# Eight adaLN tiles taken from the first layer's down projection and given to the second layer's gates and attention projection

## The chip, the core and the metric

The kernel runs on one core of a Trainium2 chip. The metric is device microseconds from the start to the end of one execution, the median of several runs. The profile is of one further execution of the same program.

## What is computed

Two layers of a decoder trunk on one sequence of 256 tokens with 1024 channels. Cut to what matters here:

```python
c_act = jax.nn.silu(c)                                   # (1, 1024)
for l in range(2):
    mod = c_act @ w_ada[l] + b_ada[l]                    # 6144 numbers out of a 1024 x 6144 matrix
    sh1, sc1, gt1, sh2, sc2, gt2 = split(mod, 6)
    h = rms_norm(x, norm_mix[l]) * (1 + sc1) + sh1
    proj = h @ w_in[l]
    # proj's columns: gated-DeltaNet q, k, v, z, a, b; attention q, k, v; gate_a; gate_b
    y_a = delta_net(...) @ w_dn_out[l]
    y_b = sliding_window_attention(...) @ w_swa_out[l]
    merged = sigmoid(gate_a) * y_a + sigmoid(gate_b) * y_b
    x = x + gt1 * (merged @ w_o[l])
    h = rms_norm(x, norm_ffn[l]) * (1 + sc2) + sh2
    up_act, up_lin = split(h @ w_up[l], 2)
    up_act = causal_dwconv(up_act, ffn_conv[l]) + ffn_conv_b[l]
    x = x + gt2 * ((silu(up_act) * up_lin) @ w_down[l])
```

All of it is float32. The line `mod = c_act @ w_ada[l] + b_ada[l]` is the adaLN modulation: six groups of 1024 numbers in each layer, which depend on `c` alone and so may be computed at any time before they are used. Groups 0 to 5 are `sh1, sc1, gt1, sh2, sc2, gt2`.

## The kernel before

**Weights.** Channels lie on the 128 partitions, tokens in the free dimension. All weights are streamed once from HBM in chunks of 128 x 1024 float32 (512 KB; 432 KB for the attention's own columns; an output tile's weights of the down projection come as three chunks, of 1024, 1024 and 768 columns). A float32 product is made of three TensorE matmuls in `float32r` (`mm3`, L262 to L265): high part times high part, high times low, low times high. So each chunk is first split: it lands in a buffer `raw`, ScalarE copies it to the high part `wH` (L192), VectorE subtracts to make the low part `wL` (L193). `emit_chunk` (L182) does this, and `weights` (L198) keeps it three chunks ahead of the chunk that TensorE multiplies (`LOOK = 3`). There are six `raw` buffers (L111), four `wH`, four `wL`.

**adaLN tiles.** `w_ada` of a layer is cut into 48 tiles of 128 x 1024 (512 KB each), eight to a group. A tile is not multiplied on TensorE: `ada_fetch` (L304) loads it into a buffer `raw` of the same six that the weights use, and `ada_dot` (L301) is one VectorE instruction (L302), which multiplies it by `silu(c)` and sums each row into one column of `modp`. After each fourth tile `ada_cols` (L319) adds the bias and makes the factors that are used later (L322 to L328). `ada_step(n)` (L337) does `n` such tiles: it issues the next loads from the list `adaq` until two are in flight, and emits the oldest one's dot product.

**When the tiles are done.** A table of numbers sets how many tiles go beside which piece of the main work. Layer 0's first 16 tiles are done at the start (`ada_first`), the other 32 in its mixer. Layer 1's 48 are done in this order: 16 in layer 0's channel sub-layer, one beside each of the hidden tiles 4 to 19 (`FST`, `FSN`, L1161); then `WDN[f]` of them beside output tile `f` of layer 0's down projection (L1176); then `ADC[1]`, nine in all, beside layer 1's convolved heads (L1060); then `GST[1]` beside each of its gate tiles (L1067); and one beside each of its attention-projection tiles (L1086), as long as the list has any:

```python
        def gate(q, f):
            ...
            ada_step(GST[l])
...
            if l + 1 < NL:
                ada_step(WDN[f])
```

Layer 1 has 12 gate tiles beside its mixer (four of `gate_a`, eight of `gate_b`; the first four of `gate_a` are done before). Groups 2 to 4 must be complete before layer 1's output projection (L1100), group 5 before its down projection (L1162).

**Order.** Each engine runs its instructions in one fixed order. It is set when the program is built: a scheduler takes instructions by priority (`tc.high_priority(offset=...)`, higher first) and by its own estimate of when each could start. The weights' splits stand above the dot products. All loads of weights and adaLN tiles are issued by SyncE's one queue, in order, and each waits there until its buffer `raw` is free, which is when the VectorE instruction that reads the buffer's last contents has run.

**The stages around the change.** Layer 0's down projection (L1165 to L1181): for each of eight output tiles, 22 blocks of the hidden vector (`g_a`, `g_b`) times three matmuls, from three chunks; then VectorE updates `x` (L1174), adds to the sum of squares (L391), and splits the next layer's input (L405). Layer 1's mixer from its gates on (L1071 to L1086): the delta rule of the second four heads (`chain_b`: a triangular inverse in steps `ps_y`, `ps_z`, then `ps_S`, `ps_KS`), and four attention units (`ps_cur`, `ps_prv`: scores; `s`, `mx`, `es`, `sme`: softmax; `ps_pT`, `pc`: transposed weights; `ps_o`: output), all woven between the matmuls of the 12 gate tiles. The attention projection (`sH`, `sL`; L1081 to L1086) can do only its first four blocks before the last attention unit is done.

Of the kernel before, what the change touches and what calls it, by code (L numbers as in the profile page):

```python
# [37 lines left out]
AHEAD = 1000  # L38
HPC = (4000, 4000)
ADC = ((2, 3, 2, 2), (3, 1, 3, 2))  # L40
GST = (1, 2)
FST = (4, 4)
FSN = ((1, 1), (1, 1))
WDN = (0, 3, 3, 3, 3, 3, 1, 0)
HPN = 20000
HPE = (500, 2000)
LAST = 2
# [52 lines left out]
def trunk(tc, xT, cvec, pos, wada, wsa, wbig, wdn, par, cst, out):  # L100
# [236 lines left out]
    def ada_step(n=1):  # L337

        for _ in range(n):
            while adaq and len(adaf) < 2:  # L340
                l, g, f = adaq.pop(0)
                adaf.append((l, g, f, ada_fetch(l, g * 8 + f)))
            if adaf:
                l, g, f, raw = adaf.pop(0)
                dot = ada_dot(l, g * 8 + f, raw)
                if behind:
                    after(dot, behind["op"])
                if f % 4 == 3:
                    ada_cols(l, g, f - 3, f + 1)
# [142 lines left out]
    for l in range(NL):  # L492
# [568 lines left out]
        def gate(q, f):  # L1061
# [3 lines left out]
            with tc.high_priority(offset=HPN):  # L1065
                A.activation(q[f // 4][:, f % 4], p_, AF.Tanh, scale=0.5)
            ada_step(GST[l])  # L1067

# [96 lines left out]
        for f in range(8):  # L1165
# [9 lines left out]
            if l + 1 < NL:  # L1175
                ada_step(WDN[f])  # L1176
                with tc.high_priority(offset=HPN):
# [92 lines left out]
```

## Time and profile before

| | us |
|---|---|
| median of 3 runs (lowest, highest) | 1035.65 (1034.38, 1040.53) |
| the profiled execution's own time | 1033.2 |
| its span (first to last instruction) | 1031.4 |
| TensorE busy | 992.9 |
| VectorE busy | 851.2 |
| ScalarE busy | 629.4 |
| adaLN dot products from `raw`, 80 of them, on VectorE | 96.9 |

Times in the trace are counted from the span's start. A row of a group says how many instructions it holds, how long the engine was busy with them, the mean of one in ns, how long the engine had stood idle just before them, and what ended the idle time. PE is TensorE, DVE VectorE, ACT ScalarE, SP SyncE, SPq its queue of DMA issues. Matmuls overlap: each takes 276 ns or so, but one starts about every 114 ns.

### The profile page before, as it was taken

How to read it: one execution, taken by the hardware profiler on the slowest of the kernel's cores; microseconds unless marked ns; L12 is line 12 of the kernel's file. 1: busy time of each engine (PE TensorE's matmuls, PEld its weight loads, DVE VectorE, ACT ScalarE, POOL GpSimd, SP SyncE). 2: the span in 40 equal slices, each digit the busy share in tenths (PEclk: the TensorE clock that was granted, in tenths of full speed). 3: DMA queues.
4: the chain of work that ended last, by engine and by line, in shares of the span. 5: the costliest groups of instructions: out<-in, count | busy, mean ns of one | idle time of the engine just before them, and what ended most of it. 6: DMA issues, size and time to landing. Idle time of an engine off the chain costs nothing.

```text
span 1031.4 us, 23285 instructions
## 1 busy us (share of the span) xinstructions
PE 992.9 (96%) x9248; PEld 950.7 (92%) x9248; DVE 851.2 (83%) x1907; ACT 629.4 (61%) x1261; POOL 4.0 (0%) x8
## 2 busy tenths in 40 slices
PE   3899999999999999999999999999999999999998
PEld 1799998997999999998999999989878999999998
DVE  6999998799788899897996999986957889777653
ACT  5389766756545675564465897667564558555532
POOL 0000000000000000000000000000000000000000
PEclk9999999999999999999999999999999999999999
DMA  9864676547566578888976547772323665666661
GB/s 358 344 225 132 228 266 223 184 136 233 161 200 186 160 230 284 272 288 260 338 286 207 169 145 224 239 252 83 97 70 103 193 195 169 198 189 196 181 211 44
DMA packets 60013, 210.48 MB, mean 204 GB/s; under 512 B 6784, under 2 KB 7808, under 8 KB 59904
## 3 DMA queue, kind: packets, MB, share of 16 engines
q1 hardware_dynamic: 59616, 208.72, 61.2%
q8 instruction: 72, 1.18, 0.5%
q14 instruction: 37, 0.30, 0.1%
q10 hardware_dynamic: 288, 0.28, 0.1%
HBM read 207.92 MB, written 1.05 MB: 203 GB/s over the span
## 4 chain that ended last, share of the span: by engine, by line
PE 66%; DVE 19%; DMA 5%; ACT 5%; issue 4%; SPq 0%; ACTq 0%; DVEq 0%
PE acc L263 18%; PE acc L264 17%; PE acc L265 17%; DVE wL L193 6%; DMA raw<-wada 4%; DVE raw L302 2%; ACT wH L192 2%; DVE kq L627 2%; DVE early L302 2%; PE pa L540 1%; PE pa L541 1%; PE ps_o L986 1%; PE ps_kk L683 1%; PE pa L539 1%; DVE vv L627 1%
## 5 line engine op out<-in xcount | busy, mean ns | idle before, releaser
L192 ACT CAST wH<-raw 128x1024 fp32r<-128x1024 f32 (+2 forms) x302 | 308.9, 1029 | 220.3 <-PE acc L264 129.8
L193 DVE TENSOR_TENSOR wL<-raw,wH 128x1024 fp32r<-128x1024 f32 (+2 forms) x302 | 359.3, 1195 | 78.0 <-ACT wH L192 75.3
L263 PE MATMUL acc<-hH,wH 128*128 128x256 f32 x1376 | 393.4, 286 | 0.0
L264 PE MATMUL acc<-hL,wH 128*128 128x256 f32 x1376 | 384.4, 279 | 0.0
L265 PE MATMUL acc<-hH,wL 128*128 128x256 f32 x1376 | 383.3, 279 | 0.0
L263 PEld LDWEIGHTS acc<-hH,wH 128*128 128x128 f32 x1376 | 258.6, 188 | 7.5 <-issue 4.1
L264 PEld LDWEIGHTS acc<-hL,wH 128*128 128x128 f32 x1376 | 258.7, 188 | 0.5
L265 PEld LDWEIGHTS acc<-hH,wL 128*128 128x128 f32 x1376 | 258.8, 188 | 0.2
L302 DVE SCALAR_TENSOR_TENSOR raw<-raw,cact 128x1024 f32<-128x1024 f32 x80 | 96.9, 1217 | 15.7 <-DMA raw<-wada 15.7
L265 PE MATMUL acc<-g_b,wL 128*128 128x256 f32 x224 | 62.3, 278 | 0.9 <-DVE wL L193 0.9
L263 PE MATMUL acc<-g_b,wH 128*128 128x256 f32 x224 | 62.0, 277 | 0.0
L264 PE MATMUL acc<-g_b,wH 128*128 128x256 f32 x224 | 62.0, 277 | 0.0
L627 DVE SCALAR_TENSOR_TENSOR kq<-cr,pt,kq 128x255 f32<-128x255 f32 (+2 forms) x96 | 45.5, 475 | 0.5 <-ACT kq L625 0.4
L265 PEld LDWEIGHTS acc<-g_b,wL 128*128 128x128 f32 x224 | 42.1, 188 | 1.3 <-DVE wL L193 1.3
L263 PEld LDWEIGHTS acc<-g_b,wH 128*128 128x128 f32 x224 | 42.0, 188 | 0.0
L264 PEld LDWEIGHTS acc<-g_b,wH 128*128 128x128 f32 x224 | 42.0, 188 | 0.0
L1147 DVE SCALAR_TENSOR_TENSOR g<-acc,pt,g 128x255 f32<-128x255 f32 x80 | 38.2, 477 | 0.6
L265 PE MATMUL acc<-g_a,wL 128*128 128x256 f32 x128 | 35.7, 279 | 2.8 <-DVE wL L193 2.8
L263 PE MATMUL acc<-sH,wH 128*128 128x256 f32 x128 | 36.6, 289 | 0.0
L265 PE MATMUL acc<-sH,wL 128*128 128x256 f32 x128 | 36.5, 287 | 0.0
L264 PE MATMUL acc<-sL,wH 128*128 128x256 f32 x128 | 36.3, 285 | 0.0
L540 PE MATMUL pa<-wL,hH 128*128 128x432 f32 x88 | 32.3, 369 | 3.7 <-DVE wL L193 3.7
(327 smaller groups left out, 1961.7 us busy)
## 6 DMA issues: line engine op xcount, KB each, us to landing
raw<-wbig SPq DMA_DIRECT2D x232, 512.0 KB, 4.1
raw<-wada SPq DMA_DIRECT2D x80, 512.0 KB, 4.5
raw<-wdn SPq DMA_DIRECT2D x32, 512.0 KB, 4.3
raw<-wsa SPq DMA_DIRECT2D x24, 432.0 KB, 6.9
early<-wada SPq DMA_DIRECT2D x16, 512.0 KB, 9.3
raw<-wdn SPq DMA_DIRECT2D x16, 384.0 KB, 4.0
x<-xT SPq DMA_DIRECT2D x4, 256.0 KB, 4.9
out<-x SPq DMA_DIRECT2D x8, 128.0 KB, 2.9
```

What stands on the lines that cost most here:

```text
L192: A.copy(h, raw)
L193: V.tensor_tensor(lo, raw, h.bitcast(F32), ALU.subtract)
L263: PE.matmul(o, wh, ah, start=first, stop=False)
L264: PE.matmul(o, wh, al, start=False, stop=False)
L265: PE.matmul(o, wl, ah, start=False, stop=last)
L302: return V.scalar_tensor_tensor(raw, raw, 1.0, cact, op0=ALU.mult, op1=ALU.mult, accum_out=modp[l][:, f:f + 1])
L539: PE.matmul(o, hh[:, kt, sl], wh[:, k4], start=kt == 0, stop=False)
L540: PE.matmul(o, hh[:, kt, sl], wl[:, k4], start=False, stop=False)
L541: PE.matmul(o, hl[:, kt, sl], wh[:, k4], start=False, stop=kt == KT - 1)
L627: V.scalar_tensor_tensor(dst[:, sft:], cr[:, :T - sft], w_[:, 3 - sft:4 - sft], dst[:, sft:], op0=ALU.mult, op1=ALU.add)
L683: PE.matmul(pk_[:, ch], t[:, 0, cs_], t[:, :, cs_], start=True, stop=True)
L1147: V.scalar_tensor_tensor(g[:, sft:], pa_[:, :T - sft], fw[:, i, 2 - sft:3 - sft], g[:, sft:], op0=ALU.mult, op1=ALU.add)
```

## The change

Two entries of the table change. Nothing else in the program's text does.

```diff
-GST = (1, 2)
+GST = (1, 1)
 FST = (4, 4)
 FSN = ((1, 1), (1, 1))
-WDN = (0, 3, 3, 3, 3, 3, 1, 0)
+WDN = (0, 1, 2, 1, 2, 1, 1, 0)
```

`WDN` now sums to 8 instead of 16, so that 24 of layer 1's tiles instead of 16 are left for its mixer. Nine of them still go beside the convolved heads. Of the others there were 7, two beside each of the first gate tiles; now there are 15, one beside each of the 12 gate tiles and one beside each of the first three tiles of the attention projection. The same 48 tiles are loaded and summed, with the same instructions.

The order in which the built program holds its instructions moves at three places. First VectorE in layer 0's down projection, at its second and third output tile (`modp_105` is layer 1's, L302 a dot product, L1174 the end of an output tile). Before:

```order
L302 SCALAR_TENSOR_TENSOR raw,modp_105<-raw,cact 128x1024 x2
L193 TENSOR_TENSOR wL<-raw,wH 128x1024
L322 TENSOR_TENSOR mod_103<-modp_105,pt 128x4
L328 TENSOR_SCALAR gt1h_112<-mod_103 128x4
L193 TENSOR_TENSOR wL<-raw,wH 128x768
L1174 SCALAR_TENSOR_TENSOR x<-acc_6461,mod_102,x 128x256
L302 SCALAR_TENSOR_TENSOR raw,modp_105<-raw,cact 128x1024
L391 TENSOR_TENSOR ssq<-ssq,sqx 128x256
L405 SCALAR_TENSOR_TENSOR xL<-x,a_1_108,xH 128x256
L193 TENSOR_TENSOR wL<-raw,wH 128x1024 x2
```

And in the change:

```order
L193 TENSOR_TENSOR wL<-raw,wH 128x1024
L302 SCALAR_TENSOR_TENSOR raw,modp_105<-raw,cact 128x1024
L193 TENSOR_TENSOR wL<-raw,wH 128x768
L1174 SCALAR_TENSOR_TENSOR x<-acc_6461,mod_102,x 128x256
L302 SCALAR_TENSOR_TENSOR raw,modp_105<-raw,cact 128x1024
L391 TENSOR_TENSOR ssq<-ssq,sqx 128x256
L405 SCALAR_TENSOR_TENSOR xL<-x,a_1_108,xH 128x256
L193 TENSOR_TENSOR wL<-raw,wH 128x1024
L322 TENSOR_TENSOR mod_103<-modp_105,pt 128x4
L328 TENSOR_SCALAR gt1h_112<-mod_103 128x4
L193 TENSOR_TENSOR wL<-raw,wH 128x1024
```

The weights' split of 1024 columns that stood behind two dot products now stands ahead of one.

Second, VectorE in layer 1's mixer, near the end of the gates (`u` and `ut` belong to the triangular inverse, `qe` to the delta rule's output, `sL` and the COPY_PREDICATED to attention). Before:

```order
L259 STREAM_TRANSPOSE ut_10343<-u_10001 128x256
L193 TENSOR_TENSOR wL<-raw,wH 128x1024 x2
L259 SCALAR_TENSOR_TENSOR u_10001<-ps_z_10387,ct,u_10001 128x8x16
L259 STREAM_TRANSPOSE ut_10444<-u_10001 128x256
L259 TENSOR_TENSOR sL<-ps_o,sH 128x4x128
L259 TENSOR_TENSOR qe<-kq,egb 128x128
L259 COPY_PREDICATED s_10440<-ct,ps_prv_10466 128x512
```

And in the change:

```order
L193 TENSOR_TENSOR wL<-raw,wH 128x1024
L302 SCALAR_TENSOR_TENSOR raw,modp_105<-raw,cact 128x1024 x2
L259 SCALAR_TENSOR_TENSOR u_9973<-ps_z_10379,ct,u_9973 128x8x16
L259 TENSOR_TENSOR sL<-ps_o,sH 128x4x128
L259 STREAM_TRANSPOSE ut_10436<-u_9973 128x256
L302 SCALAR_TENSOR_TENSOR raw,modp_105<-raw,cact 128x1024 x2
L259 TENSOR_TENSOR qe<-kq,egb 128x128
L322 TENSOR_TENSOR mod_103<-modp_105,pt 128x4
L259 COPY_PREDICATED s_10432<-ct,ps_prv_10458 128x512
```

Four dot products now stand between steps of the inverse and of the last attention unit. The others that come to the mixer stand further ahead, in the first half of the gates.

Third, TensorE at the same place, where the gates (`hH`) end and the attention projection (`sH`) begins; `ps_cur` is the last attention unit's first step. Before:

```order
L265 MATMUL acc<-hH,wL 128x256
L971 MATMUL ps_pT<-ct,s_10113 128x128 x4
L742 MATMUL ps_y_10352<-ut_10343,lq 32x32 x32
L986 MATMUL ps_o<-pc,vtok 64x512
L749 MATMUL ps_z_10387<-u_10001,yt_10385 32x32 x32
L986 MATMUL ps_o<-pc,vtok 64x512
L930 MATMUL ps_cur_10430<-kT,qT 128x128 x4
L263 MATMUL acc<-sH,wH 128x256
```

And in the change:

```order
L971 MATMUL ps_pT<-ct,s_10091 128x128 x4
L264 MATMUL acc<-sL,wH 128x256
L265 MATMUL acc<-sH,wL 128x256
L742 MATMUL ps_y_10344<-ut_10335,lq 32x32 x17
L971 MATMUL ps_pT<-ct,s_10092 128x128 x4
L742 MATMUL ps_y_10344<-ut_10335,lq 32x32 x15
L986 MATMUL ps_o<-pc,vtok 64x512
L749 MATMUL ps_z_10379<-u_9973,yt_10377 32x32 x32
L986 MATMUL ps_o<-pc,vtok 64x512
L930 MATMUL ps_cur_10422<-kT,qT 128x128 x4
```

The two transposes `ps_pT`, the inverse's step and with them the last attention unit's `ps_cur` now come after 12 matmuls of the attention projection, which stood behind them before.

## The prediction

> **What bounds the kernel now.** I read the page first, then the two down projections side by side, then who waited for whom in the first of them.
>
> ```profile
> span 1031.4 us, 23285 instructions
> PE 992.9 (96%) x9248; PEld 950.7 (92%) x9248; DVE 851.2 (83%) x1907; ACT 629.4 (61%) x1261; POOL 4.0 (0%) x8
> ```
>
> TensorE works nearly all the time, so a change that leaves its matmuls alone can win only where it stands idle: 38.5 us of the span in all, the start included. The first and last matmuls of each layer's down projection (the tiles `g_a` and `g_b`, in a window on each layer) say how much of that lies in the stage that the change relieves. Layer 0:
>
> ```profile
> L263 PE MATMUL acc<-g_a,wH x64: 276/278/332, 462.5 to 523.1; 128*128 128x256 f32 x64
> ...
> L265 PE MATMUL acc<-g_b,wL x112: 276/276/393, 465.6 to 528.1; 128*128 128x256 f32 x112
> ```
>
> Layer 1, the same 528 matmuls with no adaLN tile beside them:
>
> ```profile
> L263 PE MATMUL acc<-g_a,wH x64: 276/276/283, 967.9 to 1022.9; 128*128 128x256 f32 x64
> ...
> L265 PE MATMUL acc<-g_b,wL x112: 276/276/278, 971.0 to 1027.9; 128*128 128x256 f32 x112
> ```
>
> Layer 0 takes 528.1 - 462.5 = 65.6 us, layer 1 takes 1027.9 - 967.9 = 60.0 us, which is one matmul each 0.114 us. So the 16 tiles beside the first cost 5.6 us of TensorE's time, and no change to this stage can win more. The waits and VectorE's groups in layer 0's window:
>
> ```profile
> PE acc L265 <- DVE wL L193: 3.6, 4, 2.0
> ```
>
> ```profile
> L193 DVE TENSOR_TENSOR wL<-raw,wH 128x1024 fp32r<-128x1024 f32 (+1 forms) x27 | 30.5, 1140 | 1.2 <-ACT wH L192 1.2
> L302 DVE SCALAR_TENSOR_TENSOR raw<-raw,cact 128x1024 f32<-128x1024 f32 x17 | 20.5, 1219 | 7.5 <-DMA raw<-wada 7.5
> ```
>
> ```profile
> 462.50:528.40 65.90, 62.29 (x532) 61.42 (x531) 57.16 (x98) 30.26 (x47) 0.96 (x1) 1.00 0.90 312
> 967.90:1028.20 60.30, 60.26 (x530) 60.06 (x528) 28.39 (x32) 21.20 (x23) 0.00 (x0) 1.00 0.47 143
> ```
>
> The last view gives length, TensorE, weight loads, VectorE, ScalarE, GpSimd, clock, DMA share, GB/s. The clock is full in both. VectorE is busy 57.2 of 65.9 us, and 7.5 of the rest it stood before a dot product whose tile had not landed. How that reaches TensorE, at the longest wait:
>
> ```profile
> 484.94 1.23 DVE L302 SCALAR_TENSOR_TENSOR raw<-raw,cact 128x1024 f32<-128x1024 f32 x1 [2.48 <-DMA raw<-wada]
> 486.09 0.08 DVE L302 DVE_READ_ACCUMULATOR raw<-raw,cact 128x1 f32 x1
> 486.09 0.42 DVE L391 TENSOR_TENSOR ssq<-ssq,sqx 128x256 f32<-128x256 f32 x1
> 486.42 0.48 DVE L405 SCALAR_TENSOR_TENSOR xL<-x,a,xH 128x256 fp32r<-128x256 f32 x1
> 486.82 2.35 DVE L193 TENSOR_TENSOR wL<-raw,wH 128x1024 fp32r<-128x1024 f32 x2
> ```
>
> ```profile
> 488.09 0.38 PE L265 MATMUL acc<-g_a,wL 128*128 128x256 f32 x1 [2.00 <-DVE wL L193]
> ```
>
> VectorE idles 2.48 us for the tile, does the dot product (1.22 us), and only then the weights' split that TensorE has been waiting for.
>
> **Term 1, the down projection.** Why the tile was late stands in SyncE's issues and the median time from issue to landing.
>
> ```profile
> 478.64 0.33 SPq L185 DMA_DIRECT2D raw<-wdn  x1
> 479.78 2.64 SPq L307 DMA_DIRECT2D raw<-wada  x3
> 486.20 3.33 SPq L185 DMA_DIRECT2D raw<-wdn  x3
> ```
>
> ```profile
> raw<-wada SPq DMA_DIRECT2D x16, 512.0 KB, 5.4
> raw<-wdn SPq DMA_DIRECT2D x12, 512.0 KB, 4.8
> ```
>
> An output tile needs three chunks, and three adaLN tiles beside it make six loads, as many as there are buffers. So at TensorE's pace, 60.0 / 8 = 7.5 us for an output tile, each buffer has to be issued, land, be read and be free again in 7.5 us. Landing alone takes 5.4, the dot product 1.2, and a weight chunk waits for ScalarE's copy and VectorE's split as well: the queue stands from 482.4 to 486.2 with nothing to issue into. With one or two tiles there are four or five loads, and a buffer has 7.5 x 6 / 4 = 11.3 or 7.5 x 6 / 5 = 9.0 us for its turn, on average 10 us over the six output tiles that carry the eight tiles. The nearest stage that shows such a turn is the channel sub-layer's first half, two chunks and one tile in each period:
>
> ```profile
> L302 DVE SCALAR_TENSOR_TENSOR raw<-raw,cact x16: 1210/1214/1219, 378.2 to 460.4; 128x1024 f32<-128x1024 f32 x16
> ...
> L302 DVE SCALAR_TENSOR_TENSOR raw<-raw,cact 128x1024 f32<-128x1024 f32 x16 | 19.4, 1214 | 0.0
> ```
>
> Its 16 dot products come each 82.2 / 15 = 5.5 us, so six loads take 11 us, and VectorE never waited there. VectorE's own work falls by 8 x (1.22 + 0.08) = 10.4 us of 57.2. So a turn of 11 us loses nothing and one of 7.5 lost 5.6 us over six output tiles. By a straight line between them the two output tiles with a turn of 9.0 lose 2 x 5.6 / 6 x (11 - 9.0) / (11 - 7.5) = 1.1 us and the four with 11.3 nothing. Bounds for what stays: 0, and 3.2 if all six lose what those two do. I take 0.6, between 0 and 1.1. Term: -5.6 + 0.6 = **-5.0 us**.
>
> **Term 2, layer 1's mixer.** It gets eight dot products more and eight loads more on SyncE's queue, alternating with weight chunks. Layer 0's mixer already runs like that: one tile at each gate and each attention projection. VectorE's dot products and TensorE's waits in that stretch (175 to 296):
>
> ```profile
> L302 DVE SCALAR_TENSOR_TENSOR raw<-raw,cact 128x1024 f32<-128x1024 f32 x19 | 23.0, 1216 | 4.4 <-DMA raw<-wada 4.3
> ```
>
> ```profile
> PE ps_pT L971 <- DVE sme L259: 0.6, 1, 0.6
> PE ps_ro L877 <- DVE ro L259: 0.2, 1, 0.2
> ```
>
> And the waits in layer 1's (683 to 802), where almost no dot product ran:
>
> ```profile
> PE ps_vt L658 <- ACT yt L259: 0.8, 1, 0.8
> PE ps_KS L824 <- ACT s L259: 0.7, 1, 0.7
> PE ps_ro L877 <- DVE ro L259: 0.5, 1, 0.5
> PE ps_S L818 <- ACT y L259: 0.4, 1, 0.4
> PE ps_prv L942 <- ACT s L259: 0.2, 1, 0.2
> ```
>
> Nineteen dot products with 4.4 us of VectorE's waiting left TensorE 0.8 us of idling; without them layer 1 idles 2.6. VectorE has room for the eight: 10.4 us against this, in the stretch where four of them now stand.
>
> ```profile
> 743.00:778.00 35.00, 33.65 (x540) 26.72 (x538) 19.57 (x52) 22.43 (x67) 0.00 (x0) 1.00 0.19 62
> ```
>
> ```profile
> 752.98 0.35 DVE L259 SCALAR_TENSOR_TENSOR u<-ps_z,ct,u 128x128 f32<-128x128 f32 x1 [0.63 <-PE ps_z L749]
> ...
> 758.25 0.74 DVE L259 COPY_PREDICATED s<-ct,ps_prv 128x512 f32<-128x512 int32 x1 [2.77 <-PE ps_prv L942]
> ...
> 764.86 0.16 DVE L259 TENSOR_TENSOR sme<-sme,es 128x4 f32<-128x4 f32 x1 [3.19 <-ACT s L259]
> ```
>
> VectorE is busy 19.6 of 35 us there. The pair that stands ahead of the COPY_PREDICATED takes 2 x 1.22 = 2.4 us of an idle 2.77. DMA moves 62 GB/s, so the tiles will have landed. But the order built on this is later in one place that matters: the last attention unit starts behind 12 more matmuls, 12 x 0.114 = 1.4 us, and the attention projection's fifth block waits for that unit's end, with those 12 matmuls no longer there to fill the time. Bounds: below, layer 1 comes down to layer 0's idling, 0.8 - 2.6 = -1.8; above, all four dot products of the tail fall on the path, 4 x 1.22 = 4.9. I take **+1.0**, somewhat under the 1.4, since other matmuls stand between the unit's steps.
>
> **Nothing else moves.** Bytes, dot products and matmuls are the same. Group 5, whose last tiles now come latest, is used only in layer 1's down projection, 200 us on. The bias additions (0.15 us each) move with their tiles, into the same idle time.
>
> Sum: -5.0 + 1.0 = -4.0 us. The profiled execution took 1033.2 by its own time (1.8 around the span), so it would take 1029.2. The runs' median, 1035.65, lies 2.45 above that execution, and the same distance gives **1031.6 us**.
>
> **Rivals.** *The stall stays.* It may hang not on how many loads are in flight but on each dot product that stands ahead of a split: landing takes 5.4 us whatever their number, and in the change each output tile still has one there. For it: VectorE waited at the first dot product of a group of three, a lone one would be such a first. Against it: the channel sub-layer's lone ones never waited. Nothing won, the mixer's +1.0 stays: 1036.6. [...]
>
> [...]
>
> *The mixer pays more than the down projection wins.* Place: VectorE between the inverse's and the attention's steps in layer 1. If each of the eight dot products delays a step for which TensorE is waiting, 8 x 1.22 = 9.8, less 5.0: +4.8, 1040.4. It decides once more than 5.0 us of them falls on the path. For it: those waits exist and no matmul covers the last unit. Against it: layer 0's 19, and VectorE's 15 us of idle time.
>
> *The mixer gains too.* Two tiles at a time no longer crowd the first gates: -5.6 - 1.8 = -7.4, 1028.3. For it, layer 0's 0.8; against it, the later start of the last unit.
>
> **How the numbers follow.** Forecast 0.60, the mixer gains 0.17, the stall stays 0.13, the mixer pays 0.10. The range takes the low end from the third rival less the 1.3 us by which the runs' lowest lies under their median, 1027.0, and the high end from both terms' upper bounds (-5.6 + 3.2 + 4.9 = +2.5), 1038.2, which leaves out the slow rival. A measurement of this kernel tells about 1% from no change, 10.4 us: faster than 1025.3 needs more than every case gives, 0.02; slower than 1046.0 needs the slow rival and more, 0.03; within 1%, 0.95.
>
> **What would show it.** In layer 0's down projection: first `g_a` to last `g_b` matmul in 60 to 61.5 us instead of 65.6 (term 1), TensorE's 3.6 us of waits for `wL` under 1, VectorE's 7.5 us before L302 under 2. In layer 1, from the first gate to the last attention projection:
>
> ```profile
> L1066 ACT ACTIVATE gate<-acc x12: 367/380/386, 688.8 to 751.0; 128x256 f32<-128x256 f32 x12
> ...
> L1085 DVE SCALAR_TENSOR_TENSOR gate<-gate,acc x8: 410/421/422, 780.0 to 801.5; 128x256 f32<-128x256 f32 x8
> ```
>
> 801.5 - 688.8 = 112.7 us should become 113 to 115, with the last unit's end (the first L1085) about 1 us later after the first gate than 91.2. The forecast is wrong if the down projection stays above 63 us, or if this stretch grows by 5 or more.

## The result and the profile after

The change is slower: 1043.22 us in the median of 20 runs (1034.67 to 1051.16) against 1035.13 for the kernel before in 20 runs beside them, a ratio of 1.0066 with the interval [1.0045, 1.0088]. The ratio leaves out three runs of the change that took over 1.5% more than its fastest, and the ratios, here and below, are not quotients of the two medians. The difference is within the 1% that was forecast as the class, but on the other side of no change, and the median lies outside the range. The profiled execution took 1047.77 us:

```profile
span 1046.0 us, 23289 instructions
PE 1005.6 (96%) x9248; PEld 960.0 (92%) x9248; DVE 851.3 (81%) x1907; ACT 628.8 (60%) x1261; POOL 4.0 (0%) x8
PEclk9999999999999999999999999989959999999999
```

The work is the same, TensorE is busy 12.7 us longer with it, and its granted clock drops in the slices about 680 and 760 us. Two stages answer for the terms of the prediction. First the down projection of layer 0, by the same rows as before:

```profile
L263 PE MATMUL acc<-g_a,wH x64: 276/278/285, 460.3 to 519.9; 128*128 128x256 f32 x64
...
L265 PE MATMUL acc<-g_b,wL x112: 276/276/392, 463.4 to 524.9; 128*128 128x256 f32 x112
```

```profile
L193 DVE TENSOR_TENSOR wL<-raw,wH 128x1024 fp32r<-128x1024 f32 (+1 forms) x25 | 28.0, 1136 | 1.7 <-ACT wH L192 1.7
L302 DVE SCALAR_TENSOR_TENSOR raw<-raw,cact 128x1024 f32<-128x1024 f32 x9 | 11.0, 1223 | 16.1 <-DMA raw<-wada 16.1
```

524.9 - 460.3 = 64.6 us, where 65.6 were and 60 to 61.5 were forecast. (To the last matmul's end it is 64.9 against 65.8; the experiments count it so.) TensorE's waits for `wL` went from 3.6 to 2.7 us only. VectorE stands 16.1 us before six of its nine dot products; it had stood 7.5 before four of 17. One of the six, and the split behind it (VectorE, in order of time):

```profile
495.65 1.23 DVE L302 SCALAR_TENSOR_TENSOR raw<-raw,cact 128x1024 f32<-128x1024 f32 x1 [2.25 <-DMA raw<-wada]
496.80 0.08 DVE L302 DVE_READ_ACCUMULATOR raw<-raw,cact 128x1 f32 x1
496.80 0.95 DVE L193 TENSOR_TENSOR wL<-raw,wH 128x768 fp32r<-128x768 f32 x1
```

SyncE had issued that tile and the next only 4 us earlier:

```profile
491.51 2.24 SPq L307 DMA_DIRECT2D raw<-wada  x2
```

The second stage is layer 1's mixer, from the first gate to the last attention projection:

```profile
L1066 ACT ACTIVATE gate<-acc x12: 365/383/392, 688.6 to 752.4; 128x256 f32<-128x256 f32 x12
...
L1085 DVE SCALAR_TENSOR_TENSOR gate<-gate,acc x8: 414/420/422, 794.5 to 816.1; 128x256 f32<-128x256 f32 x8
```

816.1 - 688.6 = 127.5 us, where 112.7 were: +14.8. That the whole span grew by 14.6, nearly the same, is partly chance: the down projection began 2.2 us earlier and was 0.9 shorter, and from its end to the first gate it took 3.0 us more (163.4 against 160.4). TensorE's waits in 675 to 817:

```profile
PE ps_vt L658 <- DVE s L259: 2.5, 1, 2.5
PE ps_z L749 <- issue: 2.4, 1, 2.4
PE ps_KS L824 <- ACT s L259: 0.7, 1, 0.7
PE ps_ro L877 <- DVE ro L259: 0.5, 1, 0.5
PE ps_y L775 <- DVE ut L259: 0.3, 1, 0.3
```

They come to 6.4 us, where the five shown of before came to 2.6. But the first and the last of them end ahead of the first gate, at 682.6 and 678.2. In the stretch itself 3.6 us stand against 1.8, so the waits explain about 2 of the 14.8. The rest stands in the clock, seventh figure of these windows, the stretch 760 to 784 and then the whole of it, and below them the same two of before:

```profile
760.00:784.00 24.00, 24.00 (x177) 20.27 (x176) 8.28 (x23) 11.18 (x33) 0.00 (x0) 0.50 0.21 76
688.60:816.50 127.90, 123.98 (x1173) 108.12 (x1172) 88.34 (x242) 70.38 (x178) 0.95 (x1) 0.91 0.37 120
```

```profile
760.00:784.00 24.00, 22.82 (x190) 19.14 (x184) 12.43 (x34) 12.60 (x35) 0.00 (x0) 1.00 0.03 5
688.80:802.00 113.20, 111.31 (x1164) 98.62 (x1164) 78.77 (x224) 69.47 (x176) 0.95 (x1) 1.00 0.30 99
```

For 24 us TensorE ran at half clock, always busy by its records, which loses 12 us by estimate: half of 24. What stands just ahead of it is a standstill inside a group of 64 small matmuls, with nothing waited for:

```profile
755.35 1.07 PE L986 MATMUL ps_o<-pc,vtok 128*64 128x512 f32 x2
756.36 0.67 PE L749 MATMUL ps_z<-u,yt 32*32 32x32 f32 x54
759.42 0.28 PE L749 MATMUL ps_z<-u,yt 32*32 32x32 f32 x10 [2.40 <-issue]
```

The median lost less than this execution: 8 us. The clock differs from run to run, and with it the time. In the next run of the change eleven executions went from 1035.4 us at a mean clock of 0.998 to 1048.1 at 0.985 (median 0.992), and 34 of the kernel before beside them from 1029.6 at 1.000 to 1043.3 at 0.987 (median about 0.9965). A straight line through each gives 1036.5 and 1032.3 at 0.998. So about 4 us of the loss are there at equal clock, and about as much, (0.9965 - 0.992) x 1040 = 4.7 us, comes as lost clock.

### The profile page after: what moved, and what is told of

Its sections match the earlier page's. It is cut to its first block, busy times and chain, and to the rows that moved or that the text cites. A ratio compares the mean times of both kernels' runs of the same rounds, so it can differ in the third digit from the quotient of the medians.

```text
span 1046.0 us, 23289 instructions
## 1 busy us (share of the span) xinstructions
PE 1005.6 (96%) x9248; PEld 960.0 (92%) x9248; DVE 851.3 (81%) x1907; ACT 628.8 (60%) x1261; POOL 4.0 (0%) x8
## 4 chain that ended last, share of the span: by engine, by line
PE 69%; DVE 17%; ACT 5%; DMA 4%; issue 4%; SPq 0%; DVEq 0%; ACTq 0%
PE acc L263 18%; PE acc L264 18%; PE acc L265 18%; DVE wL L193 6%; DMA raw<-wada 4%; DVE kq L627 2%; ACT wH L192 2%; DVE early L302 2%; DVE raw L302 1%; PE ps_o L986 1%; PE ps_cur L930 1%; PE ps_kk L683 1%; DVE vv L627 1%; PE pa L540 1%; PE pa L541 1%
## 5 line engine op out<-in xcount | busy, mean ns | idle before, releaser
L302 DVE SCALAR_TENSOR_TENSOR raw<-raw,cact 128x1024 f32<-128x1024 f32 x80 | 97.1, 1218 | 24.9 <-DMA raw<-wada 24.7
L264 PE MATMUL acc<-mL,wH 128*128 128x256 f32 x128 | 35.7, 279 | 0.1
```

Source lines behind the costliest of these rows:

```text
L264: PE.matmul(o, wh, al, start=False, stop=False)
L302: return V.scalar_tensor_tensor(raw, raw, 1.0, cact, op0=ALU.mult, op1=ALU.mult, accum_out=modp[l][:, f:f + 1])
```

## The experiments

Each was timed against the kernel before on the same chip. "The mixer" below is the stretch from the first gate's start to the end of the last attention projection in the profile; it was 113.2 us in the kernel before and 127.9 in the change, counted so.

**The change again**, for a second profile.

> The changed kernel once more, for a second profile. Theory (the time went into the mixer of layer 1: a halved TensorE clock in its tail, and a few waits): the median falls again within 1040 to 1047 us, run by run lower where the granted clock is near 1.0 (about 1036) and higher where it is below 0.99 (1043 to 1051); the down projection of layer 0 takes 64 to 65.5 us in this profile too, and VectorE's waits before its nine dot products come to 14 to 18 us. Rival (the first profile caught an accident): the down projection comes out at 60 to 62 us and the stretch from the first gate to the last attention projection at 113 to 115, with the clock at 0.998.

1042.41 us, ratio 1.0066 [1.0037, 1.0095]. Down projection 66.3 us with 16.3 us of waits before the dots, mixer 126.3, a standstill of 1.8 us in L749 that ends at 760.7, and 20.5 us at half clock from 762.8 on. So each part of the first profile came again, the down projection somewhat longer than the 64 to 65.5 expected.

**One entry at a time.**

```diff
-WDN = (0, 1, 2, 1, 2, 1, 1, 0)     # run 1
+WDN = (0, 3, 3, 3, 3, 3, 1, 0)
-GST = (1, 1)                       # run 2
+GST = (1, 2)
```

> One tile per gate in layer 1, but 16 tiles beside the down projection of layer 0 as before: the mixer's queue then holds 7 tiles, which stand at the first seven gates, and nothing beside the attention projection. Theory (what costs is work of VectorE and SyncE that reaches into the late part of the mixer, where TensorE waits for the attention's and the inverse's steps): the tail is bare, so the stretch from the first gate to the last attention projection takes 112 to 115 us, the down projection 65 to 66, the whole 1034 to 1037 us. Rival (the rhythm of one tile per gate costs at the first gates already): the stretch takes 118 or more, the whole 1040 or more.

1037.58 us, ratio 1.0030 [1.0002, 1.0059], mixer 114.5. The median is just above the first theory's bound: one tile per gate costs something already with seven tiles, 0.30%, barely clear of nothing, and less than the rival wants.

> Eight tiles beside the down projection as in the change, but still two per gate in layer 1: 15 tiles stand at the first eight gates, none at the last four and none beside the attention projection. Theory A (late tiles cost, by their place): the stretch from the first gate to the last attention projection takes 113 to 117 us and the whole 1033 to 1037. Theory B (each tile more in this mixer costs, wherever it stands): the stretch takes 122 to 128 and the whole 1040 to 1045. Both have the down projection of layer 0 at 64 to 65.5 us. If my prediction's reasoning by buffers held after all, it would come out at 60 to 62.

1036.72 us, ratio 1.0019 [0.9995, 1.0043], mixer 116.5, down projection 66.0. Eight more tiles at two per gate, all within the first eight gates, cost little: theory A. The buffers' theory of the prediction failed again: 66.0, not 60 to 62.

**Dot products behind the splits, in the change.** `behind["split"]` is VectorE's split of the newest chunk whose load has been issued.

```diff
-        V.tensor_tensor(lo, raw, h.bitcast(F32), ALU.subtract)
+        behind["split"] = V.tensor_tensor(lo, raw, h.bitcast(F32), ALU.subtract)
...
+                if "late" in behind:
+                    after(dot, behind["split"])
...
             if l + 1 < NL:
+                behind["late"] = 1
                 ada_step(WDN[f])
+                del behind["late"]
```

> The change with one thing more: in the down projection of layer 0 each dot product is ordered on VectorE behind the split of the newest chunk whose load has been issued, so no split stands behind a dot product that waits for its tile. Loads, buffers and their number are those of the change. Theory (the dot product stands in VectorE's order ahead of splits, and waits a landing time there): VectorE's waits before L302 fall from 16 us to under 4, the down projection goes from 64.9 us to 60 to 61.5, and the whole from 1043 to 1038 to 1040 us. Rival (buffers: a raw tile is held longer when its dot product is later, so weight loads come later): the down projection stays at 64 or more, with TensorE waiting for wL or wH, and the whole at 1043 or above.

```profile
L264 PE MATMUL acc<-g_a,wH x64: 276/276/283, 462.5 to 517.5; 128*128 128x256 f32 x64
...
L266 PE MATMUL acc<-g_b,wL x112: 276/276/278, 465.6 to 522.5; 128*128 128x256 f32 x112
```

522.5 - 462.5 = 60.0 us, 60.2 to the last matmul's end (the file's lines have moved on by one or two): the full 5.6 won, with 1.7 us of VectorE's waiting left. Same loads, same buffers, another order on VectorE, and TensorE's order is the change's. The median is 1040.46, ratio 1.0033 [0.9999, 1.0066], so only 2 us of the gain show in it: seven of its twelve runs had a clock of 0.987 or less, and the profiled one 13.7 us at half clock from 681, behind a wait of 2.2 us for `s`. A straight line through its runs gives 1032.2 us at a clock of 0.998, 4.3 below the change's 1036.5, so at equal clock most of the gain is there.

**The same order in the kernel before**, whose six loads fill six buffers.

```diff
-GST = (1, 1)
+GST = (1, 2)
-WDN = (0, 1, 2, 1, 2, 1, 1, 0)
+WDN = (0, 3, 3, 3, 3, 3, 1, 0)
```

> The kernel before (16 tiles beside the down projection, two per gate) with one thing changed: in the down projection of layer 0 each dot product is ordered behind the split of the newest chunk whose load has been issued. Six loads still share six buffers in the output tiles that carry three tiles. Theory (order, not buffers): the down projection of layer 0 falls from 65.8 us to 60 to 61.5, VectorE's waits before L302 from 7.5 to under 3, the whole from about 1034 to 1027.5 to 1029.5. My prediction's theory (six loads in six buffers lose 5.6 us by themselves): the down projection stays at 64 to 66 and the whole at 1033 to 1036, since a dot product that comes later holds its buffer longer.

1035.67 us, ratio 1.0007 [0.9978, 1.0035], down projection 64.7: here the prediction's theory is right. The dot products wait for nothing, but ScalarE waits for the weights:

```profile
ACT wH L193 <- DMA raw<-wdn: 15.6, 9, 4.4
```

```profile
L303 DVE SCALAR_TENSOR_TENSOR raw<-raw,cact 128x1024 f32<-128x1024 f32 x18 | 21.6, 1217 | 0.0
```

In the kernel before it had waited as long already, beside the 7.5 us of VectorE:

```profile
ACT wH L192 <- DMA raw<-wdn: 16.2, 6, 5.1
```

The change's first profile has no such wait. With four or five loads in the new order it is this:

```profile
ACT wH L193 <- DMA raw<-wdn: 1.5, 1, 1.5
```

So the down projection had two limits: six loads in six buffers, and dot products ahead of splits. In these profiles taking away either wins about 1 us at most, and both 5.6 us.

**The order in the mixer too**, in the change and in the kernel before:

```diff
+        if l:
+            behind["late"] = 1
         for j in range(4):
             for which in range(3):
                 hb.conv(j, which)
...
+        behind.pop("late", None)
         finish(chain_b)
```

> The change with the dot products behind the newest issued chunk's split both in the down projection of layer 0 and in the mixer of layer 1, from its second half's convolutions to the end of the attention projection. Theory (one mechanism in both places: a dot product that waits for its tile stands ahead of a split and of the attention's scores): TensorE's wait of 2.2 to 2.8 us before ps_vt at the first gate falls to under 1.2, the clock's dip there is gone or one window of 3.4 us, the down projection takes 60 to 61.5, and the median 1031 to 1036 us. Rival (in the mixer it is VectorE's time for the dot products that costs, not their waiting): the wait before ps_vt stays over 2 and the median at 1038 to 1041, as with the down projection alone.

1036.30 us, ratio 1.0022 [0.9990, 1.0054]. The median is 4 us below that with the down projection alone, the ratio only 0.1%, so the gain is not settled. The wait of 2.2 to 2.8 us ahead of the first gate is down to 0.2, though an earlier one, for `vv`, grew from 0.6 to 1.5. The mixer still takes 124.6, with a standstill of 1.9 us in L751 and 13.7 us at half clock in two stretches.

> The kernel before with the same order in both places. Theory: the down projection takes 60 to 61.5 us as in the run with that place alone; the mixer of layer 1, whose seven tiles cost TensorE 0.8 us at most in the kernel before, stays at 112 to 114 us; the whole 1027 to 1029.5, within 1 us of the run with the down projection alone. Rival (ordering dots late in the mixer delays tiles into its tail): the mixer grows by 2 or more and the whole is over 1030.

1035.24 us, ratio 1.0010 [0.9976, 1.0043], mixer 114.8. The theory's 1027 to 1029.5 rested on a down projection of 60 to 61.5; it took 65.5, as above. The mixer is 1.6 us longer than in the kernel before, with both the theory and the rival missed by a little.

> Eight tiles beside the down projection, two per gate in layer 1 (so none at the last four gates nor beside the attention projection), and all dot products behind the newest issued split. Theory (dot products early in the mixer and none in its tail cost least): down projection 60 to 61 us, first gate to last attention projection 113 to 117, median 1028 to 1032. Rival (two dot products behind each split hold their buffers longer, so the weights of the next gate come late, as in the down projection with three tiles): the stretch takes 118 or more, the median 1034 to 1038.

1040.62 us, ratio 1.0068 [1.0045, 1.0091], mixer 126.1, the rival's side and beyond its 1038. But the weights are not what comes late: TensorE waits 0.9 us for `wH`, and longest for attention and the inverse:

```profile
PE ps_y L744 <- DVE nm L260: 3.7, 1, 3.7
PE ps_pT L973 <- DVE s L260: 2.4, 2, 1.7
```

Ahead of the wait of 1.7 us five dot products stand between the softmax's steps on VectorE. Ahead of the one of 3.7 us stands none, only a long row of small steps of both. So behind the splits is the right place beside the down projection, and not everywhere.

**The standstill.** In the change's profile TensorE stood 2.40 us, up to 759.42. A queue that the profile calls instruction moved 72 packets in the span:

```profile
q8 instruction: 72, 1.18, 0.5%
```

One landed from 756.96 to 757.89, as the standstill began. Whether the two belong together, and what TensorE stood for, is not shown. To see whether it stands at the same place with more matmuls in its order, and what the clock does if it does not, I added matmuls ahead of the mixer.

```diff
+        for _ in range(extra.pop("n", 0)):
+            PE.matmul(p_[:, 0:32], wh[:, 0], ah(0)[:, 0:32], start=True, stop=True)
         for kt in range(KT):
             mm3(p_, wh[:, kt], wl[:, kt], ah(kt), al(kt), kt == 0, kt == KT - 1)
```

> The change with 64 narrow matmuls more (32 columns, into a bank that the next matmul overwrites) in the channel sub-layer of layer 0, 300 us ahead of the mixer of layer 1. [...] They cost 1 to 3 us where they stand. [...]

In its profile the mixer has no standstill, 3.4 us at half clock in its tail, and takes 118.1 us. But the 64 narrow matmuls took 10.3 us where they stand (395.2 to 405.5), with the clock at half for 10.2 us from 398.9, and the down projection began 10 us later; the median is 1050.58, ratio 1.0151 [1.0104, 1.0198], and the comparison is spoilt. Next, 32 matmuls on constants at the very start of TensorE's order, in the change, in the change with all dots behind splits, and in the kernel before. Theory B, of the first of these runs, is that the change's new order on TensorE brings the half clock with or without a standstill.

```diff
+        pw = acc(32, name="pw")
+        for _ in range(32):
+            PE.matmul(pw, C("ident"), C("ident", 0, 32), start=True, stop=True)
```

> [...] All other engines' orders are those of the change. [...] Theory B (the order by itself): 17 to 24 us at half clock stay in the tail and the median is 1041 to 1045.

> The change with all dot products behind the newest issued split (down projection of layer 0 and mixer of layer 1) and the 32 small matmuls at the start. [...]

> The kernel before with the same 32 small matmuls at the start. [...]

These matmuls were not free: 64 records, one each 0.21 us from 6.1 us on, so that the first norm came 10 us late; the last run's trace has no standstill. With that in all three (shifted, below), 1050.46 for the change, 1044.23 with all dots behind splits, 1044.61 for the kernel before. The second run's mixer took 120.0 us with 6.8 at half clock, and it is level with the shifted kernel before. The change's profiled execution has no standstill and took 1043.55, as much as the shifted kernel before (1043.59). The down projection and the mixer, first of the change, then of the kernel before, both shifted:

```profile
471.40:533.60 62.20, 60.99 (x532) 60.59 (x531) 47.06 (x75) 28.59 (x44) 0.96 (x1) 1.00 0.82 267
695.30:812.00 116.70, 113.75 (x1175) 99.44 (x1173) 88.31 (x242) 70.39 (x178) 0.95 (x1) 1.00 0.40 132
```

```profile
471.80:536.00 64.20, 61.48 (x532) 60.68 (x531) 56.27 (x96) 29.18 (x46) 0.96 (x1) 1.00 0.91 319
697.20:811.80 114.60, 112.69 (x1174) 99.83 (x1173) 78.82 (x224) 69.51 (x177) 0.95 (x1) 1.00 0.30 98
```

So with the clock full in both stages the change wins 2.0 us in the first and loses 2.1 in the second. (The run with 64 matmuls has 62.2 in the down projection too. VectorE still waits 12.8 and 13.3 us there, TensorE only 1.2 and 1.0 for the splits; why the shift helps is not known.) Yet the median of the change's six shifted runs lies 5.9 us above that of the shifted kernel before, where 8.7 were between the two kernels unshifted (six and five runs, and their intervals [1.0119, 1.0198] and [1.0061, 1.0135] overlap). So these medians do not settle what the standstill is worth. Theory B's half clock is not in the mixer of the one execution that has a profile, though the median of the runs, 1050.46 with the 10 us of the added matmuls in it, lies above its 1041 to 1045.

**The eight tiles out of the mixer.** Group 5 is used only by layer 1's down projection. Held back, its eight tiles run beside the blocks of layer 1's channel sub-layer, and the mixer has its old seven tiles.

```diff
-GST = (1, 1)
+GST = (1, 2)
...
-            while adaq and len(adaf) < 2:
+            while adaq and len(adaf) < 2 and not (hold and adaq[0][1] == 5):
...
+        hold[:] = [l] * l        # at the start of a layer
...
+        hold.clear()             # before the channel sub-layer's loop
         gp = []
```

> The same without the new order in the down projection: the change with only one thing undone, the eight tiles in the mixer of layer 1. TensorE's order is word for word that of the kernel before. Theory: down projection 64 to 66.5 us (nothing won), the mixer 113 to 115 us, the median 1032 to 1036, level with the kernel before; the 8 to 9 us of the change are then all the mixer's. Rival (part of the change's loss lies outside the mixer): 1038 or more.

1036.87 us, ratio 1.0009 [0.9988, 1.0029], down projection 64.9: level with the kernel before. The mixer's 116.9 us lie above the 113 to 115 expected, with 10.2 us at half clock from 683.7, so this execution lost some clock too. Undone are the eight tiles' place, the one tile per gate, and with them TensorE's new order, which by the tiles' names in the trace is that of the kernel before again. So the loss comes with the eight tiles in the mixer. That their dot products cost it, and not TensorE's new order, is not shown. Nor does their number alone do it: eight tiles more, at two per gate, came to 0.19%, seven at one per gate to 0.30%, and both together, the change, to 0.66%.

> Eight tiles beside the down projection as in the change, with the dot products there behind the newest issued split; the eight tiles that this leaves over (group 5, used only by layer 1's down projection) wait for layer 1's channel sub-layer and run one beside each of its blocks, so that the mixer of layer 1 has seven tiles, two per gate, as in the kernel before. Theory (the down projection can win its 5.6 us, and the change's loss is the eight tiles in the mixer): down projection 60 to 61 us, first gate to last attention projection 113 to 115, from there to layer 1's down projection 166 to 166.6 as before, the median 1027 to 1030 us against about 1034 for the kernel before. Rival (the lost clock comes with the shorter down projection, wherever the eight tiles go): the median at 1034 or more, with half clock of 7 us or more in the mixer.

> The best of the earlier runs once more: 1029 to 1032 us in the median, the ratio to the kernel before 0.993 to 0.997, whose interval leaves out 1.

Both are one kernel. With the down projection's dot products behind the splits as well, 1030.70 us, ratio 0.9940 [0.9918, 0.9962], and on another chip 1030.04, ratio 0.9959 [0.9932, 0.9986]: faster than both kernels. Its mixer took 115.4 and 114.8 us. The two stages in the second profile, and the eight tiles in the channel sub-layer (803 to 960), before which VectorE never waits:

```profile
683.80:798.60 114.80, 112.58 (x1176) 99.74 (x1176) 78.11 (x221) 69.48 (x176) 0.95 (x1) 1.00 0.30 97
461.30:521.50 60.20, 60.20 (x532) 60.20 (x531) 47.60 (x76) 30.44 (x46) 0.96 (x1) 1.00 0.86 281
```

```profile
L303 DVE SCALAR_TENSOR_TENSOR raw<-raw,cact 128x1024 f32<-128x1024 f32 x8 | 9.8, 1220 | 0.0
```

**Which place in the mixer costs**, with the down projection at 60 us in all.

```diff
         finish(att)
+        hold.clear()             # eight beside the attention projection
...
         yb = [None, None]
+        hold.clear()             # or: one at each of the last eight gates
...
-            ada_step(GST[l])
+            ada_step(GST[l] if hold or not l else 1)
```

> As the first of these three, but the eight tiles stand one beside each block of layer 1's attention projection; the seven others two per gate. Theory (tiles in the mixer's tail stand ahead of the last attention unit's and the inverse's steps): first gate to last attention projection 117 to 123 us, half clock of 7 us or more in the tail, the median 4 to 9 us above the first of these three. Rival (what costs is a tile at each gate, and beside the attention projection there is room): the stretch 113 to 116 us, the median within 2 us of the first of these three.

1032.54 us, ratio 0.9965 [0.9944, 0.9987], mixer 117.3: 1.8 us above the best version beside it, with overlapping intervals: the rival, though the stretch is slightly over its bound.

> As where the eight tiles of group 5 stood beside the attention projection (1032.5 us in the median, dot products of the down projection behind splits), but now one at each of the last eight gates. Theory (the place that costs is the last gates, where the attention's units and the inverse take turns on VectorE): first gate to last attention projection 119 to 126 us, the median 1037 to 1042, near the 1040.5 of the change with the same order in the down projection. Rival (what costs in the change is one tile instead of two at the first gates): the stretch 115 to 118, the median 1031 to 1034.

1034.64 us, ratio 1.0001 [0.9968, 1.0034], 4.6 above the best version beside it, whose interval it touches: between the two theories. Its profile shows in small what the change's shows, a mixer of 124.3 us, a standstill and 13.7 us at half clock:

```profile
PE ps_z L753 <- issue: 1.1, 1, 1.1
PE acc L264 <- ACT gate L1070: 1.1, 1, 1.1
PE ps_vt L662 <- DVE s L260: 1.0, 1, 1.0
```

```profile
758.90:772.60 13.70, 13.70 (x99) 12.00 (x98) 4.56 (x14) 6.39 (x20) 0.00 (x0) 0.50 0.01 1
```

One per gate at the first gates, the rest of what the change does in the mixer, cost 0.30% or 3 us with seven tiles. Together that would be 4.6 + 3 = 7.6 us, against 0.66% - 0.09% = 0.57%, 5.9 us, between the change and the run with the eight tiles out of the mixer. Neither part is well clear of noise, and that they add up is not shown.

> The best of the earlier runs (eight tiles beside the down projection behind the splits, group 5 in layer 1's channel sub-layer) with the seven dot products of the mixer of layer 1 behind the newest issued split too. Theory: TensorE's wait of 2.0 us before ps_vt at the first gate goes to under 1 us and the clock's dip of 3.4 us there with it, so the median falls by 1 to 3 us against the best, to 1028 to 1030. Rival (later dot products only move the wait, as where two per gate stood behind splits): the same or up to 3 us slower.

1031.12 us, ratio 0.9997 [0.9963, 1.0032], no better than the best version. In its profile the wait of 2.0 us before `ps_vt` is down to 0.2, while the earlier one for `vv` grew from 0.6 to 1.6: the rival's way. No half clock at all lies in the mixer; but three of its twelve runs had a clock of 0.988 or less, at 1039.8 to 1043.5 us.

## Why the prediction was wrong

**Term 1, -5.0 us, measured as -0.9 and +0.5 us** in the two profiles of the change, and as -2.0 in the shifted pair. The step that failed is "a turn of 11 us loses nothing and one of 7.5 lost 5.6". It read the loads rightly: with four or five of them no weights come late, and with six they do, even when no dot product waits (64.7 us). It left out that a dot product whose tile is late holds the splits behind it, however few the loads. With the same loads and buffers and the dot products behind the splits the stage took 60.2 us instead of 64.9. The rival *the stall stays* said this and had 0.13. The evidence I set against it, that the channel sub-layer's lone dot products never waited, does not carry over: there `after(dot, behind["op"])` (L347) puts each dot product behind the current block's last VectorE instruction (L1159), and by then its tile has landed. In the change's profile one such tile was issued at 395.8, and its dot product came 6.3 us later:

```profile
401.40 0.42 DVE L1159 TENSOR_TENSOR g_b<-g,g_b 128x256 fp32r<-128x256 f32 x1
...
402.12 1.22 DVE L302 SCALAR_TENSOR_TENSOR raw<-raw,cact 128x1024 f32<-128x1024 f32 x1
```

In the down projection that instruction is still the channel sub-layer's last, long done, and orders nothing. Two lines of the program told the stages apart, and I took one as the other's model for its turn of 11 us alone.

**The signs that I named** came out as said for a wrong forecast: VectorE's waits rose to 16.1 where under 2 was right, the stage stayed above 63, and the mixer grew by 14.8 where 5 was the limit.

**Term 2, +1.0 us, measured about +6 in the median** (the change against the run with the eight tiles elsewhere), +14.8 in the profiled run. The term was built from time on VectorE's path, with an upper bound of 4.9, and at full clock that was not far off: +2.1 in the profiles of the shifted pair. The step that failed is that all of TensorE's work was priced at the full clock, as the profile of before shows it, and lost clock has no term. In the profiled run about 12 of the 14.8 us are lost clock and 2 are waits. Layer 0's mixer, which carries 19 dot products with its clock full in both profiles, was no model for this.

The longest of the change's waits, ahead of the first gate, shows a dot product at fault in part: it and a split stood ahead of attention's `s` until 681.8, and TensorE stood 2.5 us where 0.8 were.

```profile
678.55 1.23 DVE L302 SCALAR_TENSOR_TENSOR raw<-raw,cact 128x1024 f32<-128x1024 f32 x1
679.70 0.08 DVE L302 DVE_READ_ACCUMULATOR raw<-raw,cact 128x1 f32 x1
680.67 1.23 DVE L193 TENSOR_TENSOR wL<-raw,wH 128x1024 fp32r<-128x1024 f32 x1 [0.89 <-ACT wH L192]
681.82 1.28 DVE L259 SCALAR_TENSOR_TENSOR s<-ct,ps_cur 128x512 f32<-128x512 f32 x2
```

But this wait does not tell the change from the others. It is as long with the eight tiles out of the mixer, in the run that is level with the kernel before:

```profile
PE ps_vt L660 <- ACT yt L259: 2.0, 1, 2.0
```

In the two profiles of the best version it is 2.0 and 1.7 us.

**The rivals.** *The mixer pays* (0.10, 1040.4) had the place and nearly the size, but as 9.8 us of dot products on the path less 5.0 won. What came has that rival's loss without the gain, so both rivals at once, though not by its mechanism. I had given each a chance as if the other term stood, and none to the two together, 1040.4 + 5.0 = 1045.4.

**Nothing else moves** held in the main: from the end of the attention projection to the end both profiles agree within 0.1 us, and the eight tiles' removal from the mixer gave the kernel before's time. The 3.0 us more between the down projection and the first gate, with 6.8 us at half clock from 681.6, were not foreseen.

**What stays open.** What starts a long stretch of half clock in one run and not in the next. In the two profiles of the change the longest follows a standstill of 2.4 and 1.8 us, and without a standstill (the two shifted runs) the mixer took 117 to 118 us. But a standstill is not enough: one of 2.0 us in layer 0's mixer, in the run with two per gate, was followed by 3.4 us at half clock, and one of 0.9 us in layer 1's, in the last run above, by none. The shifted change lost clock in other runs all the same, and no more than one or two runs of each kernel have a profile. Open, too, is whether the dot products on VectorE or TensorE's new order make the mixer lose clock: no run has the one without the other.

## What to carry to other kernels

Before a stage serves as a model for another, compare what orders the instructions there, not only how many loads and buffers share the time: a dot product whose input is issued late stood here ahead of the splits and held them. Work that is moved to make room goes where the main engine runs long matmuls without waiting and the moved work's result is not needed soon: here the same eight tiles cost nothing that the runs can tell beside the channel sub-layer, about 2 us beside the attention projection and about 5 at the last gates, the last two close to noise. And look at the clock of each run before calling a difference explained: in the change's profile lost clock was 12 of the mixer's 14.8 us, and between its fastest and slowest run of eleven, 1035.4 and 1048.1 us, the mean clock went from 0.998 to 0.985.

## What the runs showed of the hardware

In the profiles of the kernel before and of the change TensorE's clock was either 1.00 or 0.50. Within the span it was at 0.50 once in the first, for 3.4 us from 49.6, and twice in the second, for 6.8 us from 681.6 and 23.9 us from 760.1. The other profiles add stretches of 10.2, 13.7 and 20.5 us. All six lengths are multiples of 3.4 us to within 0.1 us. Gaps of 1.1 to 2.4 us on TensorE stood ahead of all four stretches of over 13 us: 2.4 ahead of 23.9, 1.8 ahead of 20.5, 2.2 and 1.1 ahead of twice 13.7. Whether the gaps brought them on is not shown, and such a gap did not always lead to one: a wait of 1.9 us at 685, in the kernel before with the new order beside the down projection, was followed by none.

For 24 us (760 to 784 in the change) the clock stayed at half although TensorE's records show no gap, while it ran 177 matmuls of 32 to 512 columns, 24 of them 256 wide. And 64 narrow matmuls (32 columns) in a dense stretch of the channel sub-layer, again with no gap in the records, took 10.3 us, and 10.2 us at half clock began within them.

In layer 1's mixer TensorE stood 0.9 to 2.4 us with nothing waited for in six of the profiles, each time inside a group of 64 matmuls of 32x32. One without a standstill took 0.75 us with its 64 weight loads (the `ps_y` from 745.37 in the kernel before). The 32 float32 matmuls added at the start left 64 matmuls and 64 weight loads in the trace, two of each for one.
